# RWKV mixer: chunk scores and transposes in a stage of their own, the two heads' scores issued as pairs

## The chip, the cores and the metric

The kernel runs on one core of one Trainium2 chip. The metric is the device time of one execution in microseconds (us). Three executions of the kernel before took 3175.26, 3166.24 and 3173.97 us; their median is 3173.97 us. All arithmetic is in fp32, or in pairs of fp32r tiles (a high and a low part), where a product is three matmuls.

## The reference, cut to what matters

Two layers are computed over 1024 tokens of width 1024. Layer 0 has one input projection that feeds two mixers, then an output projection, an MLP and a gated embedding. Layer 1 has a chunked attention in the mixers' place. The change is in one of layer 0's mixers, RWKV-7: 8 heads of 64, one state matrix per head, updated token by token:

```python
def step(state, inp):
    r_t, w_t, k_t, v_t, a_t, b_t = inp
    sa = jnp.einsum('bhij,bhj->bhi', state, a_t)
    state = state * w_t[:, :, None, :] + sa[..., None] * b_t[:, :, None, :] + v_t[..., None] * k_t[:, :, None, :]
    return state, jnp.einsum('bhij,bhj->bhi', state, r_t)
```

The kernel computes this in chunks of 128 tokens. In a chunk, products of the decayed b and k with the decayed a and r, masked to the causal part, stand for what the tokens of the chunk do to each other: these are the chunk's scores. One of them (b with a) has to be inverted as a triangular matrix; the other three (b with r, k with a, k with r) are used as they are. Only the state goes from chunk to chunk.

## The kernel before, in words

**Units and stages.** Layer 0's mixers are cut into 16 units, RWKV and the other mixer (gated DeltaNet, "gdn") by turns. A unit of RWKV is a pair of heads (128 partitions, 64 for each head) and half of the sequence (512 tokens, 4 chunks). Each unit goes through the stages `in` (the projection, dense matmuls of 128x512), `front` (decays, the products to invert, the first part of the inverse, which goes through DRAM and GpSimd), `mid` (the rest of the inverse on TensorE, in the PSUM tile `iz`), `back` (the recurrence over the four chunks) and `post` (the norm and the gate).

**Lanes and the planner.** Each stage is a Python generator, a lane, that walks through the units (`l0_lane`, L542). A `yield` with a name stands for a wait whose length is in the table `LAT`; a `yield` with a tuple waits until another lane has marked that key. `run` (L128) keeps a clock of its own, to which every matmul adds an estimated cost (`mm`, L165), and always resumes the first lane in its list that is due; the lane of the dense projection is the last, so it fills what the others leave. The scheduler behind it then orders the instructions of each engine with a timeline of its own, and every engine runs its instructions in that order. `together` (L182) ties a list of matmuls to be issued in the order of the list.

**Back of RWKV (L913).** Before the first chunk it computes the scores of chunk 0 for both heads, and the transposes of `Bt` and `Kt` to token-major (`Btm`, `Ktm`, copied by ScalarE at L942). The helper `scores(c, h)` (L922) multiplies 64 rows of one head: `Bt` with one 128-column half of `AR`, `Kt` with both halves (256 columns), into one PSUM tile `pm`, and VectorE multiplies the 384 columns with the mask into a tile `PMQ` (L930). Then, for each chunk c: the masked state `Sh`, the product `pw` (PSUM `ch`), its copy `W` on ScalarE (L962), the scores of chunk c+1 for head 0; the product with the inverse and `U` on VectorE (L970); the state update and the outputs (`py`), `S2` on VectorE (L986), the scores of chunk c+1 for head 1.

**PSUM.** Of the 8 banks the dense projection has two (`dps`), `tp` (shared by `front` and `post`, named `tp` or `pp`, `sc`, `st`) has two, and `iz`, `pm`, `ch` and `y` have one each. At the very start three of them (`y`, `ch`, `pm`) are lent to the dense projection.

In the profile every matmul has the line L175 and every transpose L190, so they are told apart by tile. An fp32 matmul is recorded as two passes, an fp32 transpose as one.

Of the kernel before, what the change touches and what calls it, by code (L numbers as in the profile page):

```python
# [8 lines left out]
F32 = mybir.dt.float32  # L9
# [3 lines left out]
ALU = mybir.AluOpType  # L13
AX = mybir.AxisListType
PSUM = bass.MemoryType.PSUM
DRAM = bass.MemoryType.DRAM

P = 128
# [3 lines left out]
HB = 512  # L22
NT = T // P
C = 128
NEG = -1.0e30
NPMQ = 4
# [3 lines left out]
L0_BACK = {"gate": 2, "b": 14, "tm": 3, "o": 3}  # L30
# [31 lines left out]
    "rwkv_back0": 0.76,  # L62
    "rwkv_back1": 1.11,
    "rwkv_back2": 0.79,
# [43 lines left out]
class Trunk:  # L108
# [393 lines left out]
    def layer0_in(self):  # L502
        nc, tc, a = self.nc, self.tc, self.a
        with ExitStack() as es:
            self.psm = es.enter_context(self.pool("psml0", space=PSUM))
            self.psf = self.pst = es.enter_context(self.pool("psfl0", 2, space=PSUM))
# [26 lines left out]
            for t in self.F.values():  # L533
                for i in range(1, 4):
                    nc.gpsimd.memset(t[32 * i:32 * i + 32, :, 32 * (i // 2 * 2):32 * i] if i % 2 else t[64:128, :, 0:64], 0.0)

            units = [(nm, p, hf) for hf in range(2) for p in range(4) for nm in ("rwkv", "gdn")]
            self.run([self.l0_lane(units, "post", "back", 0), self.l0_lane(units, "back", "mid", 0), self.l0_lane(units, "mid", "front", 2),
                      self.l0_lane(units, "front", "in", 0, 0, 2), self.l0_lane(units, "front", "in", 0, 1, 2),
                      self.gdn_cums(), self.l0_in(units)], ahead=(1, 2))  # L540

    def l0_lane(self, units, stage, before, slack, start=0, step=1):  # L542

        follow = {"front": "mid", "mid": "back"}
        for u, (nm, p, hf) in list(enumerate(units))[start::step]:
            yield (before, u)
            if slack and u >= slack:

                yield (follow[stage], u - slack)
            if stage == "front" and u >= 4:  # L550
                yield ("post", u - 4)
            self.unit = u
            st, sc = self.state[u]
            r = yield from getattr(self, f"{nm}_{stage}")(p, hf, sc, st, u)
            if r is not None:
                self.state[u] = (r, sc)
            self.mark((stage, u), self.lat.get("end_" + stage, 0.0))
# [7 lines left out]
    def l0_in(self, units):  # L565
        nc, a, fr = self.nc, self.a, self.fr
        self.state = {}
        self.xg = []
        for u, (nm, p, hf) in enumerate(units):
            if u % 8 == 0:  # L570
# [74 lines left out]
        pt = [self.pair(k) for k in range(2)]  # L645
        sc = [self.pair(q, F32) for q in (2, 3)]
# [150 lines left out]
    def rwkv_front(self, p, hf, sc, raws, u):  # L797
        nc, h2, fr, sm, psm = self.nc, self.h2, self.fr, self.sm, self.psm
        V, A, G = nc.vector, nc.scalar, nc.gpsimd
        t2 = self.t2  # L800
# [15 lines left out]
        sq = t2()  # L816
# [44 lines left out]
        Bt, Kt = t2(tag="b"), t2(tag="b")  # L861
# [46 lines left out]

    def rwkv_mid(self, p, hf, sc, st, u):
        yield from self.inverse_end(st["X"], st["N"], 8, self.F[8])  # L910
        return dict(st, F=self.F[8])

    def rwkv_back(self, p, hf, sc, st, u):  # L913
# [3 lines left out]
        ee, cc, AR, Bt, Kt, X, Vt = (st[n] for n in ("ee", "cc", "AR", "Bt", "Kt", "F", "Vt"))  # L917
        hs = [slice(0, 64), slice(64, 128)]

        pmq = {}  # L920

        def scores(c, h):  # L922

            sl = hs[h]
            ps = psm.tile([P, 3, P], F32, tag="pm", name="pm")
            self.mm(ps[:, 0, :], Bt[sl, c * C:(c + 1) * C], AR[sl, c, 1, :], start=True, stop=True)
            self.mm(ps[:, 1:3, :], Kt[sl, c * C:(c + 1) * C], AR[sl, c].rearrange("p a t -> p (a t)"),
                    start=True, stop=True)
            d = h2.tile([P, 3, P], F32, tag="PMQ", name="PMQ", bufs=NPMQ)
            V.tensor_tensor(d, ps, self.mask3, op=ALU.mult)  # L930
            pmq[c, h] = d
        scores(0, 0)
        yield "rwkv_back0"
        scores(0, 1)
        yield "rwkv_back1"
        tm = []
        for src in (Bt, Kt):
            pt = psm.tile([P, 4, P], F32, tag="pm", name="pm")
            for c in range(4):
                self.tr(pt[:, c, :], src[:, c * C:(c + 1) * C], self.ident)  # L940
            d = t2([P, 4, P], "tm")
            A.copy(d, pt)  # L942
            tm.append(d)
            yield "rwkv_back2"
        Btm, Ktm = tm
# [3 lines left out]
        for c in range(4):  # L949
# [8 lines left out]
            for h in range(2):  # L958
                self.mm(pw[:, hs[h]], pmq[c, h][:, 1, :], Vt[:, c, hs[h]], start=h == 0, stop=False)
# [3 lines left out]
            if c < 3:  # L963
                scores(c + 1, 0)
# [16 lines left out]
            for v, j in ((Vt[:, c], 2), (U, 0)):  # L981
                for h in range(2):
                    self.mm(py_c[hs[h]], v[:, hs[h]], pmq[c, h][:, j, :], start=False, stop=j == 0)
# [4 lines left out]
            if c < 3:  # L988
                scores(c + 1, 1)
# [1008 lines left out]
```

## Time and profile before

| what | value |
|---|---|
| median of three runs | 3173.97 us |
| lowest, highest | 3166.24, 3175.26 us |
| the profiled execution's own time | 3175.69 us |
| its span (first to last instruction) | 3174.0 us |
| TensorE matmul busy | 3057.5 us (96%) |
| VectorE busy | 2018.1 us (64%) |
| ScalarE busy | 1387.8 us (44%) |
| GpSimd busy | 536.1 us (17%) |
| granted TensorE clock, mean | 0.973 |

PE is TensorE's matmul side, PEld its weight loads, DVE VectorE, ACT ScalarE, POOL GpSimd, SP the queue that issues most DMAs. A row of a group ends with what its engine was idle for just before, and what ended that idle time. The start of one matmul group to the start of the next is the time that it holds the engine; the duration shown with it is longer, since ends overlap with the next group. The stage that the change touches lies between about 60 and 940 us of the span; layer 0's MLP and layer 1 follow.

### The profile page before, as it was taken

The page shows a single profiled execution, that of the slowest core. Times are in us where ns is not written, and L with a number is a line of the kernel's source. Part 1 is how long each engine was busy: PE and PEld are TensorE (multiplying, and loading weights), DVE is VectorE, ACT ScalarE, POOL GpSimd, SP SyncE. Part 2 cuts the span into 40 slices and gives each one's busy share as a digit, 9 for nine tenths or more (in the row PEclk, how much of TensorE's full clock was granted, in tenths as well). Part 3 has the DMA queues.
Part 4 walks back from the last instruction along what each step waited for, and adds up shares of the span by engine and source line. Part 5 has one row for each costly group of instructions (what it writes and reads, how often), then busy time and mean ns, then how long its engine had stood idle before and what let it go on. Part 6 is the DMA issues. An engine that isn't in the chain of part 4 may idle for free.

```text
span 3174.0 us, 46034 instructions
## 1 busy us (share of the span) xinstructions
PE 3057.5 (96%) x17576; PEld 2523.9 (80%) x17576; DVE 2018.1 (64%) x4020; ACT 1387.8 (44%) x2640; POOL 536.1 (17%) x978
## 2 busy tenths in 40 slices
PE   7999999999999999999999989999999999999999
PEld 5777777777778888888887888888788888888887
DVE  6546666567849666655556576776769666655552
ACT  4323433333427554311223577777757555312221
POOL 6524443444500000000005111110200000000002
PEclk8989999999999999999999999999999999999999
DMA  3212112112345333522213100110255332522213
GB/s 128 77 48 64 50 43 85 54 57 64 126 153 209 136 120 112 190 93 100 99 54 129 58 32 33 47 39 16 76 197 205 136 120 107 199 93 93 107 47 106
DMA packets 144716, 309.60 MB, mean 98 GB/s; under 512 B 40944, under 2 KB 43120, under 8 KB 144496
## 3 DMA queue, kind: packets, MB, share of 16 engines
q1 hardware_dynamic: 126064, 273.10, 25.1%
q10 hardware_dynamic: 18432, 33.56, 2.7%
q8 instruction: 138, 2.26, 0.3%
q14 instruction: 82, 0.67, 0.1%
HBM read 232.16 MB, written 74.45 MB: 97 GB/s over the span
## 4 chain that ended last, share of the span: by engine, by line
PE 79%; DVE 10%; ACT 4%; DMA 4%; issue 2%; POOL 1%; SPq 0%; DVEq 0%; POOLq 0%; ACTq 0%
PE dps L175 67%; PE ch L175 2%; PE po L175 1%; PE pm L175 1%; PE iz L175 1%; PE tp L175 1%; DVE ptile L348 1%; PE pt L190 1%; DVE f L1056 1%; DMA wraw<-in_w_out 1%; PE sn L175 1%; DMA wraw<-in_w_qkv 1%; DVE wlo L302 1%; DVE pb L1838 1%; POOL subt L413 1%
## 5 line engine op out<-in xcount | busy, mean ns | idle before, releaser
L175 PE MATMUL dps<-r,act 128*128 128x512 f32 x3528 | 824.4, 392 | 0.0
L175 PEld LDWEIGHTS dps<-r,act 128*128 128x128 f32 x3528 | 662.2, 188 | 145.6
L175 PE MATMUL dps<-xg,whi 128*128 128x512 f32 x1280 | 437.9, 423 | 16.2 <-ACT xg L350 7.1
L175 PE MATMUL dps<-late,act 128*128 128x512 f32 x1536 | 352.9, 391 | 0.0
L175 PEld LDWEIGHTS dps<-late,act 128*128 128x128 f32 x1536 | 288.5, 188 | 63.1
L1495 POOL TENSOR_TENSOR pn<-pn,prs 128x512 f32<-128x512 f32 x32 | 47.1, 1475 | 1621.3 <-ACT prs L384 1527.3
L175 PE MATMUL dps<-wq,act 128*128 128x384 f32 x1536 | 304.8, 343 | 8.0 <-DVE vs L1747 4.2
L175 PEld LDWEIGHTS dps<-xg,whi 128*128 128x128 f32 x1280 | 237.2, 197 | 67.0 <-ACT xg L350 7.1
L175 PEld LDWEIGHTS dps<-wq,act 128*128 128x128 f32 x1536 | 264.5, 190 | 12.6 <-DVE vs L1747 7.0
L175 PE MATMUL dps<-xg,wlo 128*128 128x512 f32 x640 | 260.4, 408 | 2.0 <-DVE wlo L302 2.0
L1371 DVE TENSOR_TENSOR late<-late,dps 128x512 f32<-128x512 f32 x224 | 152.7, 684 | 152.4 <-PE dps L175 120.3
L1470 DVE TENSOR_TENSOR xw<-xw,dps 128x512 f32<-128x512 f32 x192 | 131.5, 685 | 154.6 <-PE dps L175 151.4
L1269 ACT CAST act<-act 128x1024 fp32r<-128x1024 f32 (+1 forms) x99 | 94.7, 963 | 282.9 <-DMA act<-in_w 119.4
L1269 ACT CAST act<-late 128x512 fp32r<-128x512 f32 x210 | 124.5, 618 | 139.5 <-PE dps L175 120.2
L1270 DVE TENSOR_TENSOR act<-late,act 128x512 fp32r<-128x512 f32 x210 | 139.7, 686 | 25.9 <-ACT act L1269 25.7
L175 PEld LDWEIGHTS dps<-xg,wlo 128*128 128x128 f32 x640 | 125.5, 196 | 33.2 <-DVE wlo L302 4.1
L301 ACT CAST whi<-wraw 128x1024 fp32r<-128x1024 f32 x78 | 81.7, 1048 | 152.7 <-PE dps L175 91.4
L175 PE MATMUL dps<-xw,act 128*128 128x512 f32 x576 | 138.9, 392 | 0.0
L175 PEld LDWEIGHTS dps<-xw,act 128*128 128x128 f32 x576 | 108.1, 188 | 24.1
L1270 DVE TENSOR_TENSOR act<-act 128x1024 fp32r<-128x1024 f32 (+1 forms) x99 | 109.9, 1114 | 18.3 <-ACT act L1269 17.2
L175 PE MATMUL po<-ptile,vs 128*128 128x256 f32 (+1 forms) x576 | 103.3, 293 | 17.5 <-DVE ptile L348 8.5
L302 DVE TENSOR_TENSOR wlo<-wraw,whi 128x1024 fp32r<-128x1024 f32 x78 | 99.3, 1274 | 27.5 <-ACT whi L301 27.1
(472 smaller groups left out, 5284.9 us busy)
## 6 DMA issues: line engine op xcount, KB each, us to landing
act<-in_w SPq DMA_DIRECT2D x68, 512.0 KB
hd<-late ACTq DMA_DIRECT2D x128, 256.0 KB
late<-in_w SPq DMA_DIRECT2D x60, 512.0 KB
wraw<-in_w_in SPq DMA_DIRECT2D x56, 512.0 KB
act<-hd SPq DMA_DIRECT2D x56, 512.0 KB
wraw<-in_w_out SPq DMA_DIRECT2D x21, 512.0 KB
wraw<-in_w_qkv SPq DMA_DIRECT2D x21, 512.0 KB
pn<-pnd SPq DMA_DIRECT2D x32, 256.0 KB
```

The source lines that it names most:

```text
L175: return self.begin(self.nc.tensor.matmul(out, lhsT, rhs, start=start, stop=stop))
L190: return self.begin(self.nc.tensor.transpose(out, in_, ident))
L301: nc.scalar.copy(hi, raw)
L302: nc.vector.tensor_tensor(lo, raw, hi.bitcast(F32), op=ALU.subtract)
L348: nc.vector.tensor_tensor(dst[:, 1, sl], src, dst[:, 0, sl].bitcast(F32), op=ALU.subtract)
L413: E.tensor_tensor(o, X[:, 0:i, i:i + 1].broadcast_to((NP, i, n)), Bq[:, i:i + 1, i + 1:16].broadcast_to((NP, i, n)), op=ALU.mult)
L1056: V.scalar_tensor_tensor(y, raws[j][:, i:i + HB], cw(i), y, op0=ALU.mult, op1=ALU.add)
L1269: A.copy(hi, s)
L1270: V.tensor_tensor(lo, s, hi.bitcast(F32), op=ALU.subtract)
L1371: V.tensor_tensor(r, t, u, op=ALU.add)
L1470: V.tensor_tensor(x[n][:, sl], x[n][:, sl], ps, op=ALU.add)
L1495: G.tensor_tensor(pn, pn, prs[:, sl], op=ALU.mult)
```

## The change

The scores and the transposes leave `rwkv_back` and become a stage of their own, `rwkv_score`, with its own lane, which visits the RWKV units alone.

- **Order.** `score` of unit u comes after `front` of u and after `back` of unit u-2; `back` of an RWKV unit waits for `score` of the unit besides `mid`.
- **Scores.** They are computed for all four chunks at once, in three groups: `Bt` with `AR` for the four chunks (8 matmuls of 128 columns), then `Kt` with `AR` for two chunks (4 matmuls of 256 columns), twice. In each group the matmuls of the two heads alternate and are tied with `together`, head 1's (partitions 64 to 127) ahead of head 0's; each head has its own bank. VectorE masks a whole bank (512 columns) at a time: six multiplies of 512 for a unit, where it had eight of 384.
- **Transposes.** The same eight, and the same two copies on ScalarE, now at the end of `score`.
- **PSUM.** `pm` is gone; `tp` has three banks, and `score` takes its banks there: eight in turn for each unit. The dense projection borrows two banks at the start.
- **SBUF.** The scores of a unit are two tiles of four chunks (one for each head, one buffer each), where four tiles of one chunk and head took turns. `Bt` and `Kt` get a tag of their own with two buffers; `tm` has two buffers instead of three.
- **The planner's table** has `rwkv_score0` to `rwkv_score2` in place of `rwkv_back0` to `rwkv_back2`.

No matmul, transpose, copy or DMA is added or left out; the number of mask multiplies goes from 64 to 48.

```diff
-NPMQ = 4
-L0_BACK = {"gate": 2, "b": 14, "tm": 3, "o": 3}
+L0_BACK = {"gate": 2, "b": 10, "bk": 2, "tm": 2, "o": 3}
...
-    "rwkv_back0": 0.76,
-    "rwkv_back1": 1.11,
-    "rwkv_back2": 0.79,
+    "rwkv_score0": 1.60,
+    "rwkv_score1": 1.60,
+    "rwkv_score2": 0.79,
...
-            self.psf = self.pst = es.enter_context(self.pool("psfl0", 2, space=PSUM))
+            self.psf = self.pst = es.enter_context(self.pool("psfl0", 3, space=PSUM))
...
             self.run([self.l0_lane(units, "post", "back", 0), self.l0_lane(units, "back", "mid", 0), self.l0_lane(units, "mid", "front", 2),
+                      self.l0_lane(units, "score", "front", 0, 0, 2),
...
+            if stage == "score" and u >= 2:
+
+                yield ("back", u - 2)
+            if stage == "back" and nm == "rwkv":
+                yield ("score", u)
...
-                    self.extra = [lambda t=t: self.psm.tile([P, HB], F32, tag=t, name="dps") for t in ("y", "ch", "pm")]
+                    self.extra = [lambda t=t: self.psm.tile([P, HB], F32, tag=t, name="dps") for t in ("y", "ch")]
...
-        Bt, Kt = t2(tag="b"), t2(tag="b")
+        Bt, Kt = t2(tag="bk"), t2(tag="bk")
...
+    def rwkv_score(self, p, hf, sc, st, u):
+
+        h2, psf = self.h2, self.psf
+        AR, Bt, Kt = (st[n] for n in ("AR", "Bt", "Kt"))
+        hs = [slice(0, 64), slice(64, 128)]
+
+        pmq = [h2.tile([P, 4, 3, P], F32, tag=f"PMQ{h}", name="PMQ") for h in range(2)]
+        ps = [psf.tile([P, 4, P], F32, tag="tp", name="sp") for h in range(2)]
+        self.together([self.mm(ps[h][:, c], Bt[hs[h], c * C:(c + 1) * C], AR[hs[h], c, 1, :], start=True, stop=True)
+                       for c in range(4) for h in (1, 0)])
+        for h in (1, 0):
+            self.nc.vector.tensor_tensor(pmq[h][:, :, 0, :], ps[h], self.mask3[:, 0:1, :].broadcast_to((P, 4, P)), op=ALU.mult)
+        yield "rwkv_score0"
+        for c2 in range(2):
+            ps = [psf.tile([P, 2, 2, P], F32, tag="tp", name="sq") for h in range(2)]
+            self.together([self.mm(ps[h][:, e].rearrange("p a t -> p (a t)"), Kt[hs[h], c * C:(c + 1) * C],
+                                   AR[hs[h], c].rearrange("p a t -> p (a t)"), start=True, stop=True)
+                           for e, c in enumerate((2 * c2, 2 * c2 + 1)) for h in (1, 0)])
+            mask = self.mask3[:, 1:3, :].rearrange("p (o a) t -> p o a t", o=1).broadcast_to((P, 2, 2, P))
+            for h in (1, 0):
+                self.nc.vector.tensor_tensor(pmq[h][:, 2 * c2:2 * c2 + 2, 1:3, :], ps[h], mask, op=ALU.mult)
+            yield "rwkv_score1"
+        tm = []
+        for src in (Bt, Kt):
+            pt = psf.tile([P, 4, P], F32, tag="tp", name="tm")
+            for c in range(4):
+                self.tr(pt[:, c, :], src[:, c * C:(c + 1) * C], self.ident)
+            d = self.t2([P, 4, P], "tm")
+            self.nc.scalar.copy(d, pt)
+            tm.append(d)
+            yield "rwkv_score2"
+        return dict(pmq=pmq, Btm=tm[0], Ktm=tm[1])
...
     def rwkv_back(self, p, hf, sc, st, u):
...
-        def scores(c, h):
-
-            sl = hs[h]
-            ps = psm.tile([P, 3, P], F32, tag="pm", name="pm")
-            self.mm(ps[:, 0, :], Bt[sl, c * C:(c + 1) * C], AR[sl, c, 1, :], start=True, stop=True)
-            self.mm(ps[:, 1:3, :], Kt[sl, c * C:(c + 1) * C], AR[sl, c].rearrange("p a t -> p (a t)"),
-                    start=True, stop=True)
-            d = h2.tile([P, 3, P], F32, tag="PMQ", name="PMQ", bufs=NPMQ)
-            V.tensor_tensor(d, ps, self.mask3, op=ALU.mult)
-            pmq[c, h] = d
...
-            if c < 3:
-                scores(c + 1, 0)
...
-            if c < 3:
-                scores(c + 1, 1)
```

More of the change, by code (lines that the diff above doesn't have):

```diff
@@ L555, in l0_lane @@
             if r is not None:
-                self.state[u] = (r, sc)
+                self.state[u] = (dict(self.state[u][0], **r) if stage == "score" else r, sc)
             self.mark((stage, u), self.lat.get("end_" + stage, 0.0))
@@ L907, in rwkv_front @@
         return dict(ee=ee, cc=cc, AR=AR, Bt=Bt, Kt=Kt, N=N, X=X, bon=bon, Vt=Vt)
+    def rwkv_score(self, p, hf, sc, st, u):
[28 more added lines that the diff above has]
+        return dict(pmq=pmq, Btm=tm[0], Ktm=tm[1])
     def rwkv_mid(self, p, hf, sc, st, u):
         yield from self.inverse_end(st["X"], st["N"], 8, self.F[8])
-        return dict(st, F=self.F[8])
+        return dict(self.state[u][0], F=self.F[8])
     def rwkv_back(self, p, hf, sc, st, u):
@@ L916, in rwkv_back @@
         t2 = self.t2
-        ee, cc, AR, Bt, Kt, X, Vt = (st[n] for n in ("ee", "cc", "AR", "Bt", "Kt", "F", "Vt"))
+        ee, cc, AR, X, Vt, pmq, Btm, Ktm = (st[n] for n in ("ee", "cc", "AR", "F", "Vt", "pmq", "Btm", "Ktm"))
         hs = [slice(0, 64), slice(64, 128)]
-        pmq = {}
-        def scores(c, h):
-            sl = hs[h]
-            ps = psm.tile([P, 3, P], F32, tag="pm", name="pm")
-            self.mm(ps[:, 0, :], Bt[sl, c * C:(c + 1) * C], AR[sl, c, 1, :], start=True, stop=True)
-            self.mm(ps[:, 1:3, :], Kt[sl, c * C:(c + 1) * C], AR[sl, c].rearrange("p a t -> p (a t)"),
-                    start=True, stop=True)
-            d = h2.tile([P, 3, P], F32, tag="PMQ", name="PMQ", bufs=NPMQ)
-            V.tensor_tensor(d, ps, self.mask3, op=ALU.mult)
-            pmq[c, h] = d
[L932 to L945, printed above, removed]
         S = self.S[f"r{p}"]
@@ L958, in rwkv_back @@
             for h in range(2):
-                self.mm(pw[:, hs[h]], pmq[c, h][:, 1, :], Vt[:, c, hs[h]], start=h == 0, stop=False)
+                self.mm(pw[:, hs[h]], pmq[h][:, c, 1, :], Vt[:, c, hs[h]], start=h == 0, stop=False)
             self.mm(pw[:, 0:P], AR[:, c, 0, :], Sf, start=False, stop=True)
@@ L982, in rwkv_back @@
                 for h in range(2):
-                    self.mm(py_c[hs[h]], v[:, hs[h]], pmq[c, h][:, j, :], start=False, stop=j == 0)
+                    self.mm(py_c[hs[h]], v[:, hs[h]], pmq[h][:, c, j, :], start=False, stop=j == 0)
             S2 = h2.tile([P, 64], F32, tag="S2", name="S2", bufs=2)
```

## The prediction

> **What bounds the kernel now.** I read the page first, then sums over stretches of the stage, then the groups of instructions, then the timeline of TensorE to the hundredth of a microsecond.
>
> ```profile
> PE 3057.5 (96%) x17576; PEld 2523.9 (80%) x17576; DVE 2018.1 (64%) x4020; ACT 1387.8 (44%) x2640; POOL 536.1 (17%) x978
> ```
> ```profile
> 60.00:860.00 800.00, 765.00 (x6394) 590.33 (x6393) 515.08 (x1174) 302.77 (x641) 327.42 (x719) 0.93 0.20 64
> 167.00:197.00 30.00, 29.39 (x310) 21.81 (x308) 9.59 (x24) 5.43 (x15) 11.60 (x37) 0.57 0.16 46
> 500.00:550.00 50.00, 50.00 (x393) 41.10 (x392) 27.85 (x54) 15.29 (x25) 8.77 (x14) 1.00 0.31 104
> 900.00:940.00 40.00, 39.12 (x232) 30.95 (x231) 19.96 (x35) 13.65 (x25) 0.00 (x0) 1.00 0.45 155
> 940.00:960.00 20.00, 17.11 (x72) 12.49 (x71) 13.28 (x28) 8.84 (x13) 0.00 (x0) 1.00 0.72 240
> ```
>
> Columns: stretch, length, busy us of PE, PEld, DVE, ACT and POOL, then the granted clock. TensorE is the bound of this stage as of the whole kernel: 765 of 800 us busy, while VectorE has 515. The dense lane fills what the recurrence leaves, up to the end (39.12 of 40 us). So a microsecond less on TensorE is a microsecond off the end, for as long as dense work is left to fill with. The clock matters too: 0.93 on average over 800 us is 800 x 0.07 = 56 us of full-speed time not granted, most of it in stretches of small matmuls (0.57 from 167 to 197 us).
>
> ```profile
> L175 PE MATMUL pm<-AR,b 64*128 64x128 f32 (+1 forms) x256 | 67.8, 391 | 4.7 <-DVE PMQ L930 4.7
> ```
>
> The scores hold TensorE for some 60 us: 8 units x 4 chunks x 2 heads = 64 bursts of four passes.
>
> **What the change takes away.** First what one burst costs, by starts:
>
> ```profile
> 591.40 0.62 PE L175 MATMUL dps<-xg,whi 128*128 128x512 f32 x2
> 591.85 0.39 PE L175 MATMUL dps<-xg,wlo 128*128 128x512 f32 x1
> 592.17 0.92 PE L175 MATMUL pm<-AR,b 64*128 64x128 f32 x4
> 593.02 0.49 PE L175 MATMUL ch<-Sh,AR 128*128 128x128 f32 x2
> ```
>
> From 592.17 to 593.02 the burst holds TensorE 0.85 us. The dense matmul ahead of it takes 0.32 us instead of (591.85-591.40)/2 = 0.23, so the entry into the 64-row shape costs 0.09 more. 64 x (0.85+0.09) = 60.2 us leave.
>
> **What it adds.** The same passes, but the two heads side by side in the array. Two rows show halves of a burst:
>
> ```profile
> 481.53 0.48 PE L175 MATMUL pm<-AR,b 64*128 64x128 f32 x2
> 481.95 0.49 PE L175 MATMUL ch<-Sh,AR 128*128 128x128 f32 x2
> ...
> 482.96 0.70 PE L175 MATMUL pm<-AR,b 64*128 64x256 f32 x2
> 483.58 0.41 PE L190 MATMUL dps<-ident,ba 8*128 8x8 f32 x4
> ```
>
> Two passes of 128 columns alone hold 0.42 us, two of 256 hold 0.62, all four 0.85. So the fixed part of a burst (drain and first weight load) is 0.42+0.62-0.85 = 0.19 us, a pass of 128 columns 0.115, a pass of 256 columns 0.215. Now the front's product of Bt with the other half of AR, which already alternates the heads over two banks:
>
> ```profile
> 279.92 1.16 PE L175 MATMUL tp<-AR,b 64*128 64x128 f32 x16
> 281.01 0.49 PE L175 MATMUL ch<-Sh,AR 128*128 128x128 f32 x2
> ```
>
> Sixteen passes hold 1.09 us. One after the other they would be 16 x 0.115 + 0.19 = 2.03; as eight pairs 8 x 0.115 + 0.19 = 1.11. The second head is free. The new first group is this very shape: 1.09. Each Kt group is eight passes of 256 columns, four pairs: 4 x 0.215 + 0.19 = 1.05. A unit: 1.09 + 2 x 1.05 = 3.19; eight units 25.5; the entries 24 x 0.09 = 2.2. Together 27.7 us. **On TensorE at full clock 60.2 - 27.7 = 32.5 us go.**
>
> **Smaller terms.**
>
> *Clock and old waits.* Bursts in a half-clock stretch are dearer, and the 67.8 us of the group against 64 x 0.92 = 58.9 us leave 8.9 us for that. In their new place, behind `front`, the clock can be either: I take half, -4 (bounds 0 and -9). The 4.7 us that TensorE waited for the mask are set against new waits for the `tp` banks, net 0 (the far bound is the third rival).
>
> *The W copy loses its cover.* Between the matmul into `ch` and the product with the inverse stood a burst; ScalarE copies W meanwhile. What hides the copy now is the dense lane. Waits of TensorE in the stage:
>
> ```profile
> PE tp L175 <- ACT N L881: 5.2, 1, 5.2
> PE ch L175 <- DVE U L970: 4.9, 5, 2.2
> PE pm L175 <- DVE PMQ L930: 4.7, 3, 2.9
> PE ch L175 <- ACT W L962: 1.4, 1, 1.4
> PE ch L175 <- ACT U L1151: 0.5, 2, 0.3
> ```
>
> The gdn recurrence has the same step without scores, and its wait (U on ScalarE) is 0.5 us over 32 chunks. Bounds: 0, and 32 x 0.85 = 27 us if nothing takes the cover's place. The nearest row says near 0; I take +2. Behind the waiting product stand the dense matmuls and the chain of the next unit.
>
> *The end of the stage.* The last RWKV unit's eight bursts now run well ahead of its recurrence, so the last stretch has up to 8 x 0.85 = 6.8 us less to do while the last chain (mid, back, post) is no shorter by as much, and from 940 to 960 us TensorE already idles 2.9 of 20 us. Bounds 0 and +6.8: I take +4.
>
> *A third bank for `front`.* Its pair of LoRA products is tied too, over both `tp` banks, and here it falls apart:
>
> ```profile
> 261.14 1.12 PE L175 MATMUL tp<-lao,wa 64*128 64x512 f32 x2
> 262.20 0.66 PE L175 MATMUL ch<-W,F 128*128 128x64 f32 x4
> 262.79 0.92 PE L175 MATMUL pm<-AR,b 64*128 64x128 f32 x4
> 263.55 1.02 PE L175 MATMUL tp<-lao,wa 64*128 64x512 f32 x2
> 264.49 0.72 PE L175 MATMUL tp<-hsel,f 128*128 128x2 f32 x5
> ```
>
> Each half holds about 1 us (261.14 to 262.20); tied, one would be free. With three banks, and `score` using them too, between 0 and eight such savings: I take -2.
>
> *At nothing.* The mask multiplies:
>
> ```profile
> L930 DVE TENSOR_TENSOR PMQ<-pm,mask 128x384 f32<-128x384 f32 x64 | 35.3, 551 | 44.2 <-PE pm L175 43.9
> L676 DVE TENSOR_TENSOR raw<-dps,acc 128x512 f32<-128x512 f32 x24 | 16.6, 690 | 24.7 <-PE dps L175 24.4
> L1056 DVE SCALAR_TENSOR_TENSOR f<-raw,vecs,f 128x512 f32<-128x512 f32 x72 | 62.1, 862 | 15.3 <-ACT f L1054 14.1
> ```
>
> 64 x 0.551 = 35.3 us become 48 x 0.690 = 33.1 us, on an engine with a third of its time free. Transposes and their copies move uncut. No DMA and no GpSimd instruction moves, so the queues of SP and POOL keep their order apart from the shift. `back` waits for `score`, but `mid` runs in the same time, after the trip through DRAM that `score` doesn't make. The dense lane's two instead of three borrowed banks at the start: the third result takes one of its own two.
>
> **Sum.** -32.5 - 4 + 2 + 4 - 2 = -32.5 us. Against the profiled execution's 3175.7 us (span 3174.0, some 1.7 us around it) this is 3143.2. The median of the runs is 1.7 us under that execution, so I predict **3142 us** for the median.
>
> **Rivals.**
>
> *1. Half of it: the pairs fall apart, or the end gives it back.* The tie orders the products but doesn't hold other work out; the rows of `lao,wa` show it broken. A group whose two banks come free apart runs its passes singly. With no pair at all, a unit costs 2.03 + 2 x (8 x 0.215 + 0.19) = 5.85 us, eight 46.8, with entries 49: -11 us, and as the smaller terms cancel, 3163. Against it: the sixteen-pass row, likewise on two of the shared banks, holds. In the same range lies the whole 6.8 us lost at the end together with a bare W copy. Between 3155 and 3168.
>
> *2. More: the clock comes up.* The stretches at half clock are those with little dense work, and serial 64-row bursts stand in them. If a third of the 56 us comes back, 3142 - 19 = 3123. For it: 0.57 in a stretch of recurrence alone, 1.00 from 500 to 550 us where it is dense. Against: `iz`, `ch` and `py` remain as small as they are, and a shorter burst leaves their share larger. The Trainium skill ("TensorE: Matmul & The Clock Gate", the section on the HAM clock gate) says that the clock is halved by default and that activity over a window of about 3.4 us releases it; the rows above agree on the two levels, and by that rule this rival would be the likeliest. I stay with the rows, which don't say what counts as active.
>
> *3. Slower: TensorE stands at the `tp` banks.* `score` takes eight banks in turn out of three, so at four points of a unit (each Kt group, each transpose) its first matmul waits until an earlier bank is masked or copied, and everything on TensorE stands behind it. Two masks take 2 x 0.69 us, and a VectorE instruction ahead of them 0.86 more: 2.2 us, where the planner leaves 1.60. At 1.6 us bare each, 4 x 8 x 1.6 = 51 us more: 3193. It decides from 32.5/32 = 1.0 us a point. For it: 2.9 us for one wait on `pm`, 5.2 us for one on `tp`. Against: TensorE waited for a mask only 3 times in 64 bursts, VectorE for the scores 43.9 us, and the planner puts dense work between the groups. The Trainium skill ("TensorEngine Tiling (Array Packing)", PSUM Bottleneck) warns of just this: tiling speeds up the matmuls and not the emptying of PSUM, which can become the bottleneck. Here a pair group of 1.05 us has masks of 1.38 us, so by the rule the stage would go at VectorE's pace; the row of 43.9 us says that VectorE has the time.
>
> *4. No change.* The planner's new order costs elsewhere what the pairs save: within 9.5 us of 3174.
>
> **How the numbers follow.** My forecast (3130 to 3155) 0.52, rival 1 0.18, rival 2 0.14, rival 3 0.09, rival 4 0.07. The range 3116 to 3168 holds the forecast, rival 1 and most of rival 2. A change under 0.3%, 9.5 us, can't be told from none. Faster: 0.52 + 0.14 + most of rival 1 (0.15) = 0.81; slower: rival 3 and 0.01 of rival 4, 0.10; same: the rest of rivals 1 and 4, 0.09.
>
> **What would show it.** In the profile after: the passes `sp` and `sq` x256 with starts in pairs, groups of 16 and 8 that hold 1.09 and 1.05 us, some 30 us busy in all where `pm` had 67.8; the last recurrence about 30 us earlier; TensorE's waits for `tp`, `sp` and `sq` under 10 us. A wait of 1 us at most groups, or single starts, would prove the size wrong; a wait on W of over 10 us in all the second term; a mean clock well over 0.93 from 60 to 860 us would mean rival 2.

## The result, and the profile after

The changed kernel takes 3210.8 us (median of four runs, 3200.3 to 3212.8) against 3174.6 us for the kernel before on the same chip: ratio 1.0113 [1.0084, 1.0141], 36 us slower. The prediction was 3142 us, with a range from 3116 to 3168. The profiled execution of the changed kernel has a span of 3211.1 us, 37.1 more than before.

The first row of the page of the changed kernel (engine, busy us, share of the span, instructions), then sums over stretches of it (columns as in the prediction):

```profile
PE 3067.3 (96%) x17576; PEld 2534.5 (79%) x17576; DVE 2016.1 (63%) x4004; ACT 1388.3 (43%) x2640; POOL 524.4 (16%) x978
```
```profile
60.00:860.00 800.00, 747.68 (x6224) 577.98 (x6224) 492.82 (x1105) 290.36 (x610) 308.35 (x700) 0.90 0.20 62
940.00:960.00 20.00, 18.97 (x97) 15.62 (x96) 6.95 (x12) 4.71 (x8) 0.00 (x0) 1.00 0.34 108
960.00:980.00 20.00, 17.07 (x72) 12.84 (x71) 12.44 (x28) 8.32 (x13) 0.00 (x0) 0.91 0.60 194
60.00:950.00 890.00, 832.76 (x6798) 644.03 (x6798) 545.10 (x1227) 319.92 (x670) 333.78 (x746) 0.90 0.22 69
```

The share of 96% is what it was. But from 60 to 860 us TensorE is busy 17 us less than before, at a clock of 0.90 instead of 0.93, and starts 170 matmuls fewer. The same sum over 60 to 950 us for the kernel before:

```profile
60.00:950.00 890.00, 850.21 (x6913) 656.28 (x6911) 562.59 (x1273) 330.33 (x687) 339.44 (x745) 0.93 0.23 75
```

Two numbers of such a row are used from here on: **idle** is 890 minus the busy time (39.8 us before, 57.2 after), and **half-clock time** is 890 times what the clock lacks, that is the full-speed time that was not granted (62 before, 89 after; the clock has two digits, so within 4.5 us). Their sum, 102 and 146, counts idle time at half clock twice; it serves to compare kernels.

What was to be made cheaper did become cheaper. Groups of the changed kernel, by line, tile and shape (count, busy us, mean ns, and the idle time ahead of them with its releaser):

```profile
L174 PE MATMUL sq<-AR,bk 64*128 64x256 f32 x128 | 30.6, 509 | 0.6 <-DVE PMQ L925 0.4
L174 PE MATMUL sp<-AR,bk 64*128 64x128 f32 x128 | 12.1, 319 | 0.8 <-DVE b L1114 0.8
L934 DVE TENSOR_TENSOR PMQ<-sq,mask 128x512 f32<-128x512 f32 x32 | 21.2, 684 | 18.0 <-PE sq L174 17.5
L925 DVE TENSOR_TENSOR PMQ<-sp,mask 128x512 f32<-128x512 f32 x16 | 10.5, 685 | 0.9 <-PE sp L174 0.8
```

The scores hold TensorE for 42.7 us instead of 67.8, and TensorE waits 1.4 us for their banks. But everything comes later: the last product with the state of the RWKV recurrence starts at 913.9 us, 29 us later than before (forecast: 30 earlier). The passes of this product, first of the changed kernel, then of the kernel before (count, shortest, median and longest ns, first and last start):

```profile
L174 PE MATMUL ch<-Sh,AR x64: 270/276/582, 145.5 to 913.9; 128*128 128x128 f32 x64
```
```profile
L175 PE MATMUL ch<-Sh,AR x64: 270/276/582, 135.5 to 884.9; 128*128 128x128 f32 x64
```

TensorE's largest waits from 60 to 950 us in the changed kernel (what waited, for which instruction: us in total, times, longest):

```profile
PE iz L174 <- ACT T L439: 9.2, 4, 2.5
PE ch L174 <- DVE Sg L1164: 8.5, 10, 2.4
PE ch L174 <- DVE U L979: 5.8, 7, 1.6
PE ch L174 <- ACT W L973: 4.2, 2, 3.4
PE iz L189 <- DVE F L472: 3.0, 3, 1.8
PE ch L174 <- DVE W L1153: 2.8, 3, 1.5
```

None of these is a wait for a score. They lie in the inverse (`iz`) and in the recurrences (`ch`), half of the latter in the other mixer's (`Sg` 8.5 us, before 0.8; its `W` 2.8). Over all such rows, small ones too, the waits of the inverse add up to 18.6 us (before 13.5) and those for `ch` to 24.7 us (before 9.0). Of the latter 12.7 us are the other mixer's (before 1.6), although its own instructions are unchanged. The timeline of TensorE in the changed kernel shows how it comes about (start, duration, group, and in brackets the idle time ahead of it):

```profile
780.69 1.16 PE L174 MATMUL sp<-AR,bk 64*128 64x128 f32 x16
781.78 0.73 PE L174 MATMUL dps<-xg,whi 128*128 128x512 f32 x2
...
784.28 1.42 PE L174 MATMUL sq<-AR,bk 64*128 64x256 f32 x8
785.63 1.05 PE L174 MATMUL tp<-hsel,f 128*128 128x2 f32 x8
789.17 0.44 PE L174 MATMUL iz<-T,Ng 32*32 32x16 f32 x32 [2.48 <-ACT T L439]
789.54 1.11 PE L174 MATMUL sq<-AR,bk 64*128 64x256 f32 x2
790.57 0.29 PE L174 MATMUL iz<-Xp,Z 32*32 32x16 f32 x2
790.79 2.07 PE L174 MATMUL sq<-AR,bk 64*128 64x256 f32 x6
792.79 1.11 PE L174 MATMUL ch<-b,PMQ 128*128 128x64 f32 x4
793.70 0.74 PE L174 MATMUL ch<-Sh,AR 128*128 128x128 f32 x2
```

The sixteen passes hold TensorE for 1.09 us (780.69 to 781.78), as predicted. But the third group follows a wait of the inverse, is split by another of its matmuls (two passes, then six), runs at half clock (2.00 us for the six), and the recurrence starts right behind it: the scores of this unit are made at the last moment, in a stretch without dense work.

Most of the loss lies inside the stage. The last transposes of layer 0's mixers (into `pp`), first of the kernel before, then of the changed kernel, start 30 us later:

```profile
L190 PE MATMUL pp<-ident,fr x32: 271/273/447, 260.6 to 946.9; 128*128 128x128 f32 x32
```
```profile
L189 PE MATMUL pp<-ident,fr x32: 270/273/323, 245.1 to 976.8; 128*128 128x128 f32 x32
```

Up to there the time of TensorE can be added up from both traces without counting anything twice: each matmul from its start to the next start, weighed by the granted clock. Its work at full speed falls by 20 us (the scores from 52.6 to 30.3), the half-clock time while it works rises by 27.5 us, and idle time by 22 us. Together that is 29.6 of the 30 us.

The other 7 us lie behind the stage. 3 of them are a wait in layer 0's MLP, at the row statistics, that the kernel before hasn't; there 24 dense passes stand in its place. First the changed kernel, then the kernel before:

```profile
1193.53 1.94 PE L189 MATMUL dps<-ident,col 128*128 128x128 f32 x8 [2.95 <-DVE col L288]
```
```profile
1159.92 5.76 PE L175 MATMUL dps<-r,act 128*128 128x512 f32 x24
1165.51 1.04 PE L190 MATMUL dps<-ident,col 128*128 128x128 f32 x8
```

### The profile page after: what moved, and what is told of

The parts are those of the page before. It is cut to its first block, busy times and chain, and to the rows that moved or that the text cites. A ratio compares the mean times of both kernels' runs of the same rounds, so it can differ in the third digit from the quotient of the medians.

```text
span 3211.1 us, 46029 instructions
## 1 busy us (share of the span) xinstructions
PE 3067.3 (96%) x17576; PEld 2534.5 (79%) x17576; DVE 2016.1 (63%) x4004; ACT 1388.3 (43%) x2640; POOL 524.4 (16%) x978
## 4 chain that ended last, share of the span: by engine, by line
PE 78%; DVE 9%; ACT 4%; DMA 4%; POOL 2%; issue 2%; SPq 0%; DVEq 0%; POOLq 0%; ACTq 0%
PE dps L174 66%; PE ch L174 2%; PE iz L174 1%; PE po L174 1%; PE tp L174 1%; POOL subt L412 1%; PE pt L189 1%; POOL sub L414 1%; PE sn L174 1%; DVE ptile L347 1%; PE sq L174 1%; PE py L174 1%; DMA z<-sub 1%; PE sc L174 1%; DVE f L1063 1%
```

## The experiments

The medians, with the ratio to the kernel before on the same chip (whose medians there lay between 3174.6 and 3180.2 us, so that differences between two rows are good to some 5 us), and idle and half-clock time worked out as above from each kernel's own row from 60 to 950 us. "Own" means that the score products have the PSUM bank `pm`, which only the scores and the transposes of their unit use; "shared" that they go through the `tp` banks of `front` and `post`, "half shared" that one head's do. The kernels with half the scores or one product for both heads leave out half of the score products, "thinner filler" a part of the dense products.

| kernel | median us | ratio | score banks | idle | half-clock | sum |
|---|---|---|---|---|---|---|
| before | 3174.6 | 1 | own | 40 | 62 | 102 |
| after | 3210.8 | 1.0113 [1.0084, 1.0141] | shared | 57 | 89 | 146 |
| early key | 3199.0 | 1.0062 [1.0044, 1.0081] | shared | 63 | 80 | 143 |
| after, untied | 3222.5 | 1.0146 [1.0126, 1.0165] | shared | 54 | 98 | 152 |
| pairs inside back, ahead of it | 3219.1 | 1.0132 [1.0110, 1.0153] | shared | 90 | 98 | 188 |
| before, nudged | 3169.9 | 0.9976 [0.9967, 0.9986] | own | 41 | 53 | 95 |
| before, scores twice | 3218.5 | 1.0123 [1.0100, 1.0146] | own | 32 | 62 | 95 |
| pairs in back's places | 3193.5 | 1.0046 [1.0029, 1.0064] | half shared | 62 | 80 | 142 |
| early, singles, own bank | 3182.9 | 1.0030 [1.0011, 1.0049] | own | 47 | 53 | 101 |
| early key, nudged | 3186.9 | 1.0038 [1.0025, 1.0050] | shared | 62 | 62 | 124 |
| early key, planner told | 3184.6 | 1.0042 [1.0025, 1.0059] | shared | 60 | 62 | 122 |
| before, other gate | 3190.5 | 1.0045 [1.0030, 1.0060] | own | 40 | 62 | 102 |
| early, told, other gate | 3180.3 | 1.0015 [0.9999, 1.0031] | shared | 50 | 62 | 112 |
| after, other gate | 3196.7 | 1.0068 [1.0044, 1.0092] | shared | 60 | 80 | 140 |
| before, half the scores | 3136.6 | 0.9867 [0.9843, 0.9890] | own | 56 | 36 | 91 |
| before, thinner filler | 3145.0 | 0.9893 [0.9872, 0.9915] | own | 39 | 62 | 101 |
| after, nudged | 3204.8 | 1.0082 [1.0059, 1.0104] | shared | 66 | 80 | 146 |
| early, told, other gate, half own | 3190.3 | 1.0035 [1.0022, 1.0048] | half shared | 66 | 62 | 128 |
| own bank, half the scores | 3149.3 | 0.9914 [0.9901, 0.9927] | own | 63 | 45 | 107 |
| early key, one product for both heads | 3185.2 | 1.0025 [1.0014, 1.0036] | shared | 69 | 71 | 140 |

**When do the scores run, and are they tied?** The key that the score lane waits for is marked by `front` with 46.33 us added on the planner's clock (the table's time for the inverse's way through DRAM). An early key leaves that out:

```diff
-                      self.l0_lane(units, "score", "front", 0, 0, 2),
+                      self.l0_lane(units, "score", "fr", 0, 0, 2),
...
+            if stage == "front":
+                self.mark(("fr", u))
```

> The changed kernel, but the score lane starts when front has issued its last instruction, not 46.33 us of the planner's clock later (that delay belongs to the inverse's trip through DRAM). Theory A (late start: score runs beside mid, right ahead of back, so it stands on the recurrence and in the stretches poor in dense work): 3150 us, between 3135 and 3170, the first scores of a unit 40 us or more ahead of its recurrence. Theory B (lost cover: the recurrence's waits have nothing to fill them any more, wherever score runs): 3200 to 3215. Theory C (any new order of the planner moves the time by about 1 per cent): anything from 3170 to 3230.

12 us less than the changed kernel, 23 more than the kernel before, and far from the 3150 us of theory A. In this kernel the first `sp` pass starts at 73.8 us instead of 131.1, and the pair groups mostly run among dense work; its timeline of TensorE and its group of `sq`:

```profile
196.15 1.13 PE L174 MATMUL sq<-AR,bk 64*128 64x256 f32 x8
197.22 0.49 PE L174 MATMUL ch<-W,F 128*128 128x128 f32 x2
...
200.49 0.70 PE L174 MATMUL sq<-AR,bk 64*128 64x256 f32 x2
201.11 0.49 PE L174 MATMUL ch<-U,b 128*128 128x128 f32 x2
201.53 1.13 PE L174 MATMUL sq<-AR,bk 64*128 64x256 f32 x6
202.59 0.49 PE L174 MATMUL po<-b,U 128*128 128x128 f32 x2
```
```profile
L174 PE MATMUL sq<-AR,bk 64*128 64x256 f32 x128 | 24.2, 426 | 0.0
```

So the second price is right too: 1.07 us for the four pairs of 256 columns (worked out: 1.05), and 35.9 us for all scores with the 11.7 us of `sp`. A group that another matmul splits loses a pair: 0.62 us for two passes, and the other six still hold 1.06. The early key takes off a third of the loss, not all of it. Of these 12 us 7 are seen in the scores themselves (35.9 against 42.7 us); the rest is no more than the order alone can do, as shown below.

The changed kernel without the tie, each group head by head:

```diff
-                       for c in range(4) for h in (1, 0)])
+                       for h in (1, 0) for c in range(4)])
```

> The changed kernel with the heads one after the other in each group of scores, so that no two passes run side by side. By the pass times 2.03 - 1.09 and twice 1.91 - 1.05, 2.7 us a unit, 21 us of TensorE more. Theory A: score stands on the recurrence, so 15 to 25 us more than the changed kernel, 3225 to 3235. Theory B: TensorE has time free there, 3205 to 3215. Theory C: no fixed sign.

12 us slower than the changed kernel, where 21 had been costed. On TensorE the pairs are a gain, but a smaller one than costed.

The pair groups moved back into `back`, ahead of the first chunk (`st = dict(st, **(yield from self.rwkv_score(p, hf, sc, st, u)))`, no score lane):

> The changed kernel without the lane: back calls score as its first step, so the pairs, the three shared banks and the whole-bank masks stay and only the separate place goes (Bt and Kt go back to the common tag, with 12 buffers). Theory A: score was on the recurrence anyway, so 3200 to 3225, about as the changed kernel. If the lane itself did the harm: 3150 to 3175. Theory B: 3205 to 3215.

8 us slower than the changed kernel. TensorE's largest waits for tiles of the pool `tp` (60 to 950 us):

```profile
PE tp L174 <- DVE b L865: 28.6, 4, 12.8
PE tp L189 <- DVE b L1112: 10.4, 2, 5.7
PE sq L174 <- DVE PMQ L931: 6.6, 2, 4.0
```

The first is not a wait for a bank: L865 writes `Bt`, which is the input of the product that waits, and in the longest of these waits TensorE goes on 0.15 us after it has ended. It shows an order that puts the product long before its input is ready, with nothing between. The other two are waits for a bank, which L1112 or the mask L931 empties: 17 us.

**How much is the order alone?** The planner's table was nudged: in the kernel before (`"rwkv_back4": 0.64` to `0.70`), in the early kernel (`"rwkv_score0"` and `"rwkv_score1"`: 1.60 to 1.20) and, later, in the changed kernel (`rwkv_back4` as before).

> The kernel before with one entry of the planner's table nudged, the wait for the W copy from 0.64 to 0.70 us. It changes nothing but the order. Theory C: 8 us or more away from the kernel before, either way. Theories A and B: within 8 us of it, 3166 to 3182.

> e1_early with two entries of the planner's table nudged, the waits behind a group of scores from 1.60 to 1.20 us. A measure of what the order alone does: theory D and the sharing of banks both give within 10 us of e1_early, 3189 to 3209; a move of 15 us or more either way would say that the planner's order outweighs the mechanisms.

> The changed kernel with the planner's wait ahead of the product with the inverse at 0.70 instead of 0.64, the same nudge that took 5 us off the kernel before by order alone. If the loss of 36 us is the luck of one order, this moves by 10 us or more either way (3200 or 3222); if it belongs to the stage's place, it stays within 6 us of 3211.

Each nudge moved the time, without a change of any product: -6, -12 and -6 us (-8, -8 and -10 by the ratios to the kernel before on the same chip). The order is worth some 10 us, and is not the 36. A difference of that size between two rows of the table shows no cause by itself.

The gate of the dense lane at the other mixer's projection (`yield ("front", u - 2)` from unit 2 on, changed to `yield ("post", u - 4)` from unit 4 on), which waits for the same delayed key, in the kernel before and in the changed one:

> The kernel before with one wait of the dense lane changed: the gate projection of unit u waits for post of u-4, which frees its buffer, and not for front of u-2, whose key comes 46.33 us of the planner's clock after front. Theory S (the stage has stretches in which the dense lane is shut out, and there TensorE has small work alone, idles and runs at half clock; what the scores' work is worth depends on these): 3140 to 3160, with fewer half-clock stretches. Theory D: 3168 to 3182.

> The changed kernel as it is, score late, with e10_gate's wait. Theory S: most of the loss goes, 3150 to 3180. Theory A (the late place on the recurrence is the harm): 3190 to 3210, as score still runs right ahead of back.

+16 us on the kernel before, -14 on the changed one. A dense lane shut out by that key is no common cause.

The early kernel with the planner told that a pair costs half (`self.now = (self.now + t0) / 2` behind each group), alone and with the other gate:

> e1_early with the planner's clock told that the two heads of a tied group run side by side (half the cost of each group). Theory P (the planner counts pairs as if one after the other, so the order it writes leaves the other lanes late): 3170 to 3188, below e1_early's 3199 by 10 us or more. Theory D (latencies of the recurrence, whatever the plan): 3192 to 3206.

> e9_told and e10_gate together: early score, tied pairs, the planner told, the dense lane not shut out. Theory S: with dense work at hand the pairs' 30 us count at last, so 20 to 35 us under e10_gate, 3110 to 3135. Theory D: within 10 us of e9_told.

-14 and another -4 us (-6 and -9 by the ratios), each no more than a nudge. This is the best of the versions with pairs, and it isn't told from the kernel before.

**Does TensorE's work set the end?** The kernel before with every score product issued twice, the planner's clock unchanged:

> The kernel before with every product of the scores issued twice into the same place, the planner's clock not told of it: 64 x 2 x (0.115 + 0.215) = 42 us of TensorE more on the places where the scores stand. If TensorE's work sets the end of the stage, as the prediction had it: 3210 to 3220. If the scores there lie in the shadow of other waits (theory D, a chain of latencies sets the stage and TensorE's work is partly fill): 3176 to 3195.

```profile
L175 PE MATMUL pm<-AR,b 64*128 64x128 f32 (+1 forms) x512 | 117.7, 373 | 5.6 <-DVE PMQ L934 5.6
```

This is the scores' group in that kernel: 50 us more busy time than 67.8 (42 us as costed ahead), and 44 us more at the end. The other direction, with half of the score work left out in place, and with the filler made thinner:

```diff
-            ps = psm.tile([P, 3, P], F32, tag="pm", name="pm")
-            self.mm(ps[:, 0, :], Bt[sl, c * C:(c + 1) * C], AR[sl, c, 1, :], start=True, stop=True)
...
+            if h == 0:
+                ps = psm.tile([P, 3, P], F32, tag="pm", name="pm")
+                pm[c] = ps
+                self.mm(ps[:, 0, :], Bt[:, c * C:(c + 1) * C], AR[:, c, 1, :], start=True, stop=True)
...
+            else:
+                ps = pm[c]
+                self.now += 2 * 384 / 1200
```

> The kernel before with half of its score work taken off TensorE in place: each chunk's products are made once, over all 128 rows (so over both heads together), and the mask multiply of the second head reads the same bank; 32 of the 64 bursts fall away, everything else and the planner's clock stay (the output is not the reference's: the scores of the two heads are mixed). It mirrors the run in which the score products were issued twice and which cost 44 us for 42 us of work. A, TensorE's work sets the end in both directions: 32 x 0.94 = 30 us less, 3175 - 30 = 3145. B, the stage sits at a balance of TensorE's work and the chains' latencies, and what is taken away comes back as waits and half-clock time: 0 to -10, 3165 to 3175. C, the new order that the scheduler makes of it costs by itself: above 3180.

```diff
-        self.mm(ps, wl, xh, start=False, stop=last)
+        if self.thin:
+            self.now += 512 / 2400
+        else:
+            self.mm(ps, wl, xh, start=False, stop=last)
...
+            self.thin = acts is self.xg and k in (3, 5)
```

> The kernel before with the filler made thinner instead of the chains: in layer 0's input projections the low-part product of the weights is left out for two of the eight blocks (some 150 passes of 512 columns at 0.23 us, 34 us; the output is less exact than the reference), the planner's clock as before. A, TensorE's work sets the end: -34, 3140. B, balance: what is taken from the filler leaves the chains' waits bare and the clock lower, so clearly less comes off: 0 to -15, 3160 to 3175, with TensorE's idle time and its half-clock time in the stage up by some 20 us together.

-43.6 and -35.2 us. For half the scores 30 us had been costed; the thinner filler has 132 passes fewer, 30 us at 0.23 us. The work taken away comes off in full, from the chains and from the filler, and from the chains more than that. The row from 60 to 950 us and the scores' group of the kernel with half the scores:

```profile
60.00:950.00 890.00, 834.11 (x6978) 658.26 (x6978) 598.24 (x1336) 364.07 (x741) 337.36 (x745) 0.96 0.27 87
```
```profile
L175 PE MATMUL pm<-AR,b 128*128 128x256 f32 (+1 forms) x128 | 29.6, 351 | 0.1
```

Its scores cost 38 us less than before (29.6 against 67.8), TensorE idles 16 us more, but the clock rises from 0.93 to 0.96, 27 us. That is rival 2's gain, in the kernel that the change was not.

**Then why does it not come off with the pairs?** Two places are left: outside the recurrence, and the shared banks. Pairs in `back`'s old places, both heads' scores of chunk c+1 in one tied burst behind the copy of W, head 1 in the old bank `pm`, head 0 in a `tp` bank:

```diff
+            ps = [self.psf.tile([P, 3, P], F32, tag="tp", name="pf"), psm.tile([P, 3, P], F32, tag="pm", name="pm")]
...
-                scores(c + 1, 0)
+                scores(c + 1)
```

> The kernel before with the scores still in the recurrence, but those of both heads of chunk c+1 tied in one burst behind the W copy, head 1 in the bank pm and head 0 in a tp bank: 32 bursts of 0.94 us in place of 64, 30 us of TensorE less, nothing moved to a stage of its own. If TensorE's work sets the end: 3140 to 3155. Theory D: 3170 to 3190, the time comes back as idle time and half clock. If it is the sharing of the tp banks that hurts: above 3190.

The place is the old one and the scores hold TensorE less (30 us as costed; 42.7 us busy in the trace against 67.8), yet it is 19 us slower, just inside the forecast for the case that sharing the `tp` banks hurts. Its row from 60 to 950 us, and TensorE's largest wait there:

```profile
60.00:950.00 890.00, 827.72 (x6843) 644.10 (x6842) 550.10 (x1245) 321.76 (x675) 330.27 (x745) 0.91 0.22 71
```
```profile
PE pp L190 <- DVE fr L1178: 10.0, 4, 3.7
```

This wait (2.1 us before) is again not one for a bank: the transposes wait for their input `fr`.

The converse, the early stage of its own with single bursts of one head and chunk in their own bank `pm`, and two `tp` banks as before:

```diff
-        ps = [psf.tile([P, 4, P], F32, tag="tp", name="sp") for h in range(2)]
...
+                ps = self.psm.tile([P, 3, P], F32, tag="pm", name="pm")
```

> e1_early (score as soon as front has issued) without pairs and without shared banks: score works in bursts of one chunk and head in the bank pm of its own, masks of 384 columns, and tp has two banks again. Sharing the tp banks is what hurts: 3150 to 3178. Theory D: sharing is not it, and without the cover inside the recurrence 3185 to 3205, with some 25 us more TensorE busy than e1_early.

8 us over the kernel before, between the two forecasts and within what an order is worth, and idle and half-clock time are as in the kernel before (101 us). Then the same with half of the work left out, and the early pair kernel with each pair replaced by one product (TensorE time as with the pairs, five shared banks a unit instead of eight):

> The version with the early key, single bursts and a bank of their own (3182.9 against 3174.6), with half of its score work left out in the same way as inside back, where that took 42 us off: one burst for both heads, the second mask reads the same bank, the planner's clock as before (the output is not the reference's). P, the place is at fault, work outside the recurrence covers nothing and its removal pays nothing: 3176 to 3186. B, the place is innocent and the loss of the pair versions is in the shared banks: the full 30 to 42 us come off, 3141 to 3153.

> The version with the early key and the pairs (3199.0), with each pair replaced by one product over all 128 rows: as many passes in time on TensorE as the pairs (8 of 0.115 us, 4 of 0.215 us a group), the same place, the same masks and the same planner's clock, but five shared banks a unit instead of eight (the output is not the reference's). B, the shared banks are what eats the gain: 3165 to 3180. P, the place or the planner's order: within 8 us of 3199.

The rows from 60 to 950 us of these three, in that order:

```profile
60.00:950.00 890.00, 842.87 (x6903) 644.88 (x6902) 556.15 (x1265) 330.54 (x685) 337.39 (x745) 0.94 0.24 74
```
```profile
60.00:950.00 890.00, 827.14 (x6882) 644.62 (x6882) 582.58 (x1305) 348.52 (x712) 337.41 (x745) 0.95 0.26 83
```
```profile
60.00:950.00 890.00, 820.93 (x6781) 643.01 (x6781) 562.41 (x1247) 329.36 (x685) 338.78 (x746) 0.92 0.24 75
```

With a bank of its own the stage keeps what is taken away: 3149.3 against 3182.9, 34 us. So the place outside the recurrence is innocent, once the key is early. Three shared banks less in the pair kernel bring 14 us (3185.2 against 3199.0), between the two forecasts; a nudge brought the same kernel 12, so this isn't told from the order. The last two have the same place and about the same score work (31.6 and 28.2 us busy), and differ by 36 us, more than any nudge: banks, and with them the size of the groups (four bursts spread over a unit against three large groups) and what goes with both, the masks and the third `tp` bank.

The best pair version with one bank of each pair, and the transposes, in the old bank `pm`:

> The version with the early key, the planner told of the pairs and the other gate for the dense lane (3180.3), now with two shared banks as in the kernel before and the old bank of its own for one half of each score pair and for the transposes. If the third shared bank is what costs some 5 us in layer 0's MLP, that goes and the time is 3174 to 3176; if it is the order, no change: 3180. If the pairs now wait for the shared bank, as the single bursts inside back did, it is above 3185.

6 us slower by the ratios than with three shared banks, 10 by the medians, no more than an order is worth. A pair then needs both banks free at once, and one transpose alone waits 10.3 us for its bank (TensorE's wait in this kernel):

```profile
PE tm L189 <- ACT tm L949: 10.3, 1, 10.3
```

No version with all of the computation beats the kernel before by more than the 0.3% that a measurement can tell; the nudged kernel before, at 0.9976 [0.9967, 0.9986], comes nearest.

## Why the prediction was wrong, point by point

**The bound.** "A microsecond less on TensorE is a microsecond off the end" was right where the rest of the stage stays as it is: +44 us for 42 added, -35 for 30 of filler, -44 for 30 of scores, where the clock rose besides. **The price of the pairs** was right for a whole group at full clock: 1.09 and 1.07 us, worked out as 1.09 and 1.05. Their sum was too low (42.7 us busy for some 30, 35.9 with the early key), for the half clock and, as rival 1 had it in part, for groups that are split: nine of the 24 are in the changed kernel. So the term of -32.5 us was too large as well. Without the entries it was 54.4 - 25.5 = 28.9 us; at full speed, from start to start, the traces have 52.6 - 30.3 = 22.3.

**The step that failed is the smaller term "clock and old waits"**, -4 us with bounds 0 and -9, and "net 0" for the waits. From 60 to 950 us idle time rose by 17 and half-clock time by 27 us; up to the end of the stage, 30 us later than before, it is 22 and 27.5 us, which outweighs the 20 us of work saved. The bounds covered only the clock of the bursts themselves; they took idle time and clock of everything else in the stage as given. A part of it was readable in the code. "Mid runs in the same time", the step at nothing, holds only if the scores start when `front` ends; the key says 46.33 us later, and so some of them ran at half clock, right ahead of the recurrence. The early key brought 12 us; 7 of these are seen in the scores' own time, the rest isn't told from the order.

**The rest goes with the shared banks, without being shown to come from them.** In the table the sum of idle and half-clock time is 91 to 107 us in all eight kernels whose scores have their own bank, with 30 us less work or 42 us more, inside `back` or outside; it is 112 to 188 in all twelve that send scores through `tp` (between 107 and 112 the clock's rounding doesn't separate them, and a nudge alone takes the early kernel from 143 to 124). Rival 3 had the place, but not the mechanism: TensorE waits 1.4 us at the score banks of the changed kernel, not 51. It stands long at shared banks only where the pairs sit in `back` (17 us). With a lane of its own the loss appears elsewhere, as waits in the inverse and both recurrences and as half clock. How a shared bank turns into those waits, by the order that the scheduler writes when it sees banks come free late, or by a later `front`, isn't shown; nor was the size of the groups separated from the banks, since a pair needs two banks at once and all eight are taken. The cause of this rest stays open.

The Trainium skill ("TensorEngine Tiling (Array Packing)", Restrictions and Gotchas, PSUM Pressure) says that row tiling raises the pressure on PSUM because row tiles must write to different banks; the table goes the same way, 101 us with one bank of its own against 143 with pairs in the shared ones. Its warning that emptying PSUM may become the bottleneck (PSUM Bottleneck) doesn't show at the scores of the changed kernel: VectorE waited 18.3 us for them, and TensorE 1.4 us for their banks. The Trainium skill ("TensorE: Matmul & The Clock Gate", A second HAM failure mode: psum-queue depth-cycling) describes, for another kernel, short idle times from cycling through banks that bring the clock down again and again. The clocks here would fit (0.89 to 0.93 shared, 0.93 to 0.96 own), but no run shows that this is the path.

**W copy:** +2 predicted; TensorE waits 4.2 us for it, 1.4 before. Right. **End of the stage:** +4 predicted; the last 20 us before layer 0's next part idle 2.9 us in both. Nothing. **Third bank:** -2 predicted for the LoRA pair, and at 3 us it costs more: the wait at the row statistics is there in each of the ten kernels with three `tp` banks and in none of the ten with two. Why it comes 200 us after the stage isn't shown.

**Rival 4**, the planner's order, is real at some 6 to 16 us, and its band of 9.5 us around no change was too narrow.

## What to carry to other kernels

When a change takes work off the bounding engine, cost it twice: the work itself, which comes off in full, and the idle and reduced-clock time of the whole stage, which rose here wherever the work went to buffers that other chains need; read the second as one number (length minus busy, plus length times missing clock) before and after. Look up what a new lane waits for, with the time that the key carries, and not only which key it is. Where a planner writes the order, a nudge of one constant tells how much of a difference is order alone (here 6 to 12 us), and a run with part of the work left out in place tells whether the bound is the bound.

## What the runs showed of the hardware

Less small work on TensorE moved its granted clock both ways: with 38 us busy of small matmuls taken out in place it rose from 0.93 to 0.96, and with 25 us taken out by the pairs it fell to 0.90. Two products of 64 rows, alternating over two banks, run side by side (1.09 us for sixteen passes of 128 columns, 1.07 for eight of 256); a split group's six passes hold 1.06 us at full clock (at 201.53 us in the early kernel) and 2.00 at half (at 790.79 us in the changed one).
